# One DMA per k-tile of B in the opening of a 4096-cubed matmul, with two tiles over SyncE and evictions moved to ScalarE

## The chip, the cores and the metric

The kernel runs on one core of one Trainium2 chip. The metric is the device time of one execution in microseconds (us). Times are medians of several runs. Profiles are one execution each; their span is about 2 us shorter than the time of the same run (1789.8 against 1791.62 us before).

PE is TensorE's matmul, PEld its weight load, DVE VectorE, ACT ScalarE, POOL GpSimd, SP SyncE. A "k-tile" is 128 of the 4096 values of K. An eviction moves finished sums out of a PSUM bank, where TensorE leaves them, into SBUF. The granted clock is the share of TensorE's full clock that the throttle let through. A packet is one record of the DMA trace: one contiguous row, for example 4 KB of B.

## The reference

```python
a: (4096, 4096) float32;  b: (4096, 4096) float32;  bias: (4096,) float32
out = tanh(a @ b + bias)          # float32
```

## The kernel before

Both matrices are rounded to fp16 by the DMA that loads them (here these are GpSimd's), A is transposed by DVE in 32x32 blocks (`QP = 32`), and TensorE runs 8,192 matmuls of 128x512 (8,224 in the profile, since the last row tile is done in two halves). K is cut into four quarters (`Q = 4`, `KQ = 1024`), and k-tile `t` consists of 32 rows from each quarter, since that is what the 32x32 transposes of A produce. So a k-tile of B lies in memory as four blocks of 32 rows, 16 MB apart.

```python
P = 128; Q = 4; QP = 32; NB = 512        # NCW = 1024 columns of B at a time, KT = 32 k-tiles
G = 4; KS = 8; WARM = 24                 # opening: two groups of 4 row tiles; k-tiles 0..7 first

def load_b(bt, n0, t0, nt, q):           # one quarter of nt k-tiles
    src = b[ds(q * KQ + t0 * QP, nt * QP), ds(n0, NCW)]
    nc.gpsimd.dma_start(
        out=bt[t0 // TB][ds(q * QP, QP), ds(t0 % TB, nt), :],
        in_=src.rearrange("(t p) n -> p t n", p=QP),         # outermost dimension: 32
    )

def load_b_all(t0, nt):
    for q in range(Q):
        load_b(b_cur, 0, t0, nt, q)

def put_aside(ps, m, j):                 # a PSUM bank of groups 0 and 1 after k-tiles 0..7
    nc.vector.tensor_tensor(
        out=aside(m, j), in0=ps, in1=bias_bc[:, ts(j, NB)], op=mybir.AluOpType.add
    )
# ... (cut)
want_a("g0a", 2, 0, 2 * Q, 0, KS)        # A, group 0, row tiles 0 and 1, k-tiles 0..7 (4 DMAs)
want(lambda: load_b_all(0, 2))
want_a("g0b", 2, 2 * P, 2 * Q, 0, KS)    # A, group 0, row tiles 2 and 3
for t in range(2, KS, 2):
    want(lambda t=t: load_b_all(t, 2))
want(lambda: load_bias(bias_bc, 0))      # 4 KB, read 128 times: 512 KB
want_a("g1a", 2, 4 * P, 2 * Q, 0, KS)
want_a("g1b", 2, 6 * P, 2 * Q, 0, KS)
for t in range(KS, KT, TA):              # the rest of K, 8 k-tiles at a time
    want_a(("g0", t), G, 0, G * Q, t, TA)
    for u in range(t, t + TA, TB):
        want(lambda u=u: load_b_all(u, TB))
# ... (cut: the loads of group 1's rest)
turn(ats[0], "g0a", 0, 0, KS)            # transposes of A
turn(ats[1], "g0a", Q, 0, KS)
across(ps, (0, 1), 0, 2, 0)              # k-tiles 0 and 1, row tiles 0 and 1
turn(ats[2], "g0b", 0, 0, KS)
turn(ats[3], "g0b", Q, 0, KS)
across(ps, (2, 3), 0, 2, 0)
across(ps, range(G), 2, KS - 4, 0)
# ... (cut: group 0 put aside; group 1 the same; then k-tiles 8..31 of both; then the steady loop)
```

While TensorE waits for the first data it runs 24 warm-up matmuls on zeros.

## Time and profile before

| | us |
|---|---|
| time, median of 4 runs (beside the changed kernel) | 1792.15 (1791.02 to 1792.79) |
| steady loop, 7,712 matmuls, busy | 1657.8 (215 ns each) |
| first real matmul | 11.35 |
| group 1 starts | 30.12 |
| k-tile 8 starts | 44.01 |
| last pair of DVE operations starts / span ends | 1785.61 / 1789.8 |

The first two lines are from the page of the kernel before: the busy time of each engine, and the chain of waits by engine. The third is the page's group for the steady loop (busy us and mean ns of one, then idle us ahead of it); the mean of one, 378 ns, includes overlap with the next, so the pace is 1657.8 / 7,712 = 215 ns.

```profile
PE 1779.1 (99%) x8248; PEld 807.4 (45%) x8248; DVE 745.0 (42%) x420; ACT 162.7 (9%) x260; POOL 358.0 (20%) x668
...
PE 95%; DMA 4%; POOL 1%; issue 1%; DVE 0%; ACT 0%; ACTq 0%; DVEq 0%; POOLq 0%
...
L321 PE MATMUL ps<-b,at 128*128 128x512 f16 x7712 | 1657.8, 378 | 0.0
```

TensorE bounds the kernel, and the steady loop has no idle time. Only the opening and the end can move. The timeline of TensorE in the opening of the kernel before has start, length, the instruction, and in brackets the idle time ahead of it and what ended it:

```profile
1.19 7.26 PE L196 MATMUL ps<-zeros 128*128 128x512 f16 x24 [1.19 <-DVE zeros L193]
11.35 3.05 PE L121 MATMUL ps<-b,at 128*128 128x512 f16 x8 [2.90 <-DMA b<-in_b_dram]
15.36 14.06 PE L121 MATMUL ps<-b,at 128*128 128x512 f16 x56 [0.95 <-DVE at L83]
30.12 14.05 PE L121 MATMUL ps<-b,atx 128*128 128x512 f16 x64 [0.71 <-DVE atx L83]
44.01 41.60 PE L121 MATMUL ps<-b,at 128*128 128x512 f16 x192
86.23 41.61 PE L121 MATMUL ps<-b,atx 128*128 128x512 f16 x192 [0.62 <-DVE atx L83]
```

The windows of the kernel before show the granted clock. The columns are the window and its length, then the busy us of PE, PEld, DVE, ACT and POOL with their instructions in brackets, then the granted clock of TensorE, the busy share of the 16 DMA engines, and GB/s written (a share above 1 means packets that overlap):

```profile
12.00:20.00 8.00, 6.96 (x20) 2.15 (x19) 2.37 (x2) 0.00 (x0) 6.50 (x13) 0.58 1.16 200
20.00:30.00 10.00, 9.41 (x44) 4.04 (x42) 3.57 (x6) 0.00 (x0) 7.64 (x14) 1.00 1.34 215
```

After the 2.9 us without work the clock is low: 0.58 on average from 12 to 20 us. Shorter windows have 0.50 from 12 to 18.7 us and 1.00 from 18.8; work had gone on at 15.36. What sets the clock's fall and its return is not shown by this trace. The DMA stream runs at about 200 GB/s written, which is half of what is read (over the whole run, 169.91 MB on the queue of the loads against 337.64 MB read from HBM), and stays there to 80 us (205 GB/s from 30 to 80 us).

### The profile page before, as it was taken

The page shows a single profiled execution, that of the slowest core. Times are in us where ns is not written, and L with a number is a line of the kernel's source. Part 1 is how long each engine was busy: PE and PEld are TensorE (multiplying, and loading weights), DVE is VectorE, ACT ScalarE, POOL GpSimd, SP SyncE. Part 2 cuts the span into 40 slices and gives each one's busy share as a digit, 9 for nine tenths or more (in the row PEclk, how much of TensorE's full clock was granted, in tenths as well). Part 3 has the DMA queues.
Part 4 walks back from the last instruction along what each step waited for, and adds up shares of the span by engine and source line. Part 5 has one row for each costly group of instructions (what it writes and reads, how often), then busy time and mean ns, then how long its engine had stood idle before and what let it go on. Part 6 is the DMA issues. An engine that isn't in the chain of part 4 may idle for free.

```text
span 1789.8 us, 19352 instructions
## 1 busy us (share of the span) xinstructions
PE 1779.1 (99%) x8248; PEld 807.4 (45%) x8248; DVE 745.0 (42%) x420; ACT 162.7 (9%) x260; POOL 358.0 (20%) x668
## 2 busy tenths in 40 slices
PE   8999999999999999999999999999999999999999
PEld 3444444444444444444444444444444444444444
DVE  5463344334433444334433443344334433444341
ACT  0110000000000000000000000000000000000001
POOL 6422222211222211111132222111111111111100
PEclk9999999999999999999999999999999999999999
DMA  9999887665777865655588777555665555655621
GB/s 182 214 189 189 155 159 147 125 132 114 159 147 144 170 140 108 121 119 124 106 168 156 158 142 142 121 112 107 127 120 112 112 113 109 125 112 111 120 70 41
DMA packets 138630, 238.26 MB, mean 133 GB/s; under 512 B 14769, under 2 KB 27569, under 8 KB 138545
## 3 DMA queue, kind: packets, MB, share of 16 engines
q0 software_dynamic: 101248, 169.91, 56.6%
q1 hardware_dynamic: 37296, 67.13, 10.3%
q8 instruction: 64, 1.05, 0.2%
q14 instruction: 22, 0.17, 0.0%
HBM read 337.64 MB, written 67.11 MB: 226 GB/s over the span
## 4 chain that ended last, share of the span: by engine, by line
PE 95%; DMA 4%; POOL 1%; issue 1%; DVE 0%; ACT 0%; ACTq 0%; DVEq 0%; POOLq 0%
PE ps L321 92%; PE ps L121 2%; DMA b<-in_b_dram 2%; DMA an<-in_a_dram 1%; POOL b L66 0%; DMA bias_bc<-in_bias_dram 0%; POOL an L75 0%; DVE atx L83 0%; ACT o_sb L135 0%; DVE o_sb L132 0%; ACTq L354 0%; DVEq L132 0%; POOLq L343 0%
## 5 line engine op out<-in xcount | busy, mean ns | idle before, releaser
L321 PE MATMUL ps<-b,at 128*128 128x512 f16 x7712 | 1657.8, 378 | 0.0
L321 PEld LDWEIGHTS <-at 128*128 128x128 f16 x7712 | 754.6, 98 | 903.3
L132 DVE TENSOR_TENSOR o_sb<-ps,bias_bc 128x512 f32<-128x512 f32 (+1 forms) x243 | 166.4, 686 | 977.8 <-PE ps L321 764.1
L83 DVE STREAM_TRANSPOSE at<-an 128x4096 f16<-128x4096 f16 (+1 forms) x136 | 551.0, 4056 | 26.7 <-DMA an<-in_a_dram 26.7
L75 POOL DMA_DIRECT2D an<-in_a_dram x524 | 282.8, 547 | 1296.6 <-DVE at L83 1224.4
L135 ACT ACTIVATE o_sb<-o_sb 128x512 f32<-128x512 f32 (+1 forms) x243 | 151.5, 624 | 1505.7 <-DVE o_sb L132 1505.7
L66 POOL DMA_DIRECT2D b<-in_b_dram x136 | 73.2, 542 | 55.2 <-PE ps L321 28.6
L121 PE MATMUL ps<-b,at 128*128 128x512 f16 x256 | 58.6, 391 | 3.9 <-DMA b<-in_b_dram 2.9
L121 PE MATMUL ps<-b,atx 128*128 128x512 f16 x256 | 55.7, 379 | 1.3 <-DVE atx L83 1.3
L121 PEld LDWEIGHTS <-at 128*128 128x128 f16 x256 | 25.3, 100 | 37.1 <-issue 5.7
L121 PEld LDWEIGHTS <-atx 128*128 128x128 f16 x256 | 24.8, 98 | 32.2 <-DVE atx L83 2.7
L132 DVE TENSOR_TENSOR spill<-ps,spill 128x512 f32<-128x512 f32 x16 | 10.7, 684 | 25.7 <-PE ps L121 25.4
L135 ACT ACTIVATE spill<-spill 128x512 f32<-128x512 f32 x16 | 10.0, 630 | 117.2 <-DVE spill L132 117.2
L83 DVE STREAM_TRANSPOSE atx<-an 128x1024 f16<-128x1024 f16 (+1 forms) x8 | 18.3, 2295 | 0.0
L155 DVE TENSOR_TENSOR spill<-ps,bias_bc 128x512 f32<-128x512 f32 x16 | 10.1, 670 | 10.0 <-PE ps L121 10.0
L196 PE MATMUL ps<-zeros 128*128 128x512 f16 x24 | 7.3, 476 | 1.2 <-DVE zeros L193 1.2
L196 PEld LDWEIGHTS <-zeros 128*128 128x128 f16 x24 | 2.8, 118 | 5.2 <-issue 2.5
L90 POOL DMA_DIRECT2D bias_bc<-in_bias_dram x4 | 2.3, 563 | 0.1
L135 ACT ACT_TABLE_LOAD x1 | 1.3, 1283 | 0.7 <-PEq L343 0.7
L193 DVE MEMSET zeros<- 128x256 uint32 x1 | 0.3, 272 | 0.9 <-PEq L343 0.9
L343 POOL MEMSET const-float32-0.0<- 128x1 f32 x1 | 0.1, 98 | 0.2 <-issue 0.2
L343 POOL MEMSET const-bfloat16-1.0<- 128x1 bf16 x1 | 0.1, 101 | 0.0
(2 smaller groups left out, 0.2 us busy)
## 6 DMA issues: line engine op xcount, KB each, us to landing
an<-in_a_dram POOLq DMA_DIRECT2D x492, 256.0 KB, 5.4
out_dram<-o_sb SPq DMA_DIRECT2D x239, 256.0 KB, 4.3
b<-in_b_dram POOLq DMA_DIRECT2D x120, 256.0 KB, 8.9
out_dram<-spill SPq DMA_DIRECT2D x16, 256.0 KB, 6.4
an<-in_a_dram POOLq DMA_DIRECT2D x16, 192.0 KB, 7.8
an<-in_a_dram POOLq DMA_DIRECT2D x16, 128.0 KB, 5.7
b<-in_b_dram POOLq DMA_DIRECT2D x16, 128.0 KB, 5.0
bias_bc<-in_bias_dram POOLq DMA_DIRECT2D x4, 512.0 KB, 8.2
```

What stands on the lines that cost most here:

```text
L66: nc.gpsimd.dma_start(out=bt[t0 // TB][ds(q * QP, QP), ds(t0 % TB, nt), :], in_=src.rearrange("(t p) n -> p t n", p=QP),)
L75: nc.gpsimd.dma_start(out=an[ds(q * QP, QP), :, :], in_=src.rearrange("(mb p) k -> p mb k", p=QP),)
L83: nc.vector.transpose(at[:, ds(t0, nt), :].rearrange("P t (mb p) -> P mb t p", p=QP), an[:, ds(mb0, Q), :].rearrange("P mb (t k) -> P mb t ...
L90: nc.gpsimd.dma_start(out=bias_bc, in_=bass.AP(tensor=src.tensor, offset=src.offset, ap=[[0, P], *src.ap]),)
L121: nc.tensor.matmul(ps, at[:, t, :], bt[t // TB][:, t % TB, ts(j, NB)], start=start, stop=stop)
L132: nc.vector.tensor_tensor(out=o_sb[:, piece], in0=ps[:, piece], in1=addend[:, piece], op=mybir.AluOpType.add)
L135: nc.scalar.activation(o_sb[:, piece], o_sb[:, piece], mybir.ActivationFunctionType.Tanh)
L155: nc.vector.tensor_tensor(out=aside(m, j), in0=ps, in1=bias_bc[:, ts(j, NB)], op=mybir.AluOpType.add)
L193: nc.vector.memset(zeros, 0.0)
L196: nc.tensor.matmul(warm, zeros[:, :P], zeros, start=i == 0, stop=i == WARM - 1)
L321: nc.tensor.matmul(ps, at[:, t, :], b_cur[t // TB][:, t % TB, ds(c0, w)], start=t == 0, stop=t == KT - 1,)
L343: nc = _bacc.Bacc("TRN2", target_bir_lowering=False, num_devices=1)
```

## The change

Its intent: start TensorE sooner. Two k-tiles of B leave at once on SyncE as float32 and are rounded by ScalarE; A is ahead of the rest of B on GpSimd; one DMA per k-tile saves GpSimd's issues (0.54 us each); ScalarE empties group 0's banks so that DVE can transpose group 1; three transposes are moved forward; the last stores leave on two queues.

```diff
+    RAW = 2
-    def put_aside(ps, m, j):
+    def put_aside0(ps, m, j):
+        nc.scalar.copy(aside(m, j), ps)
+    def add_bias(m, j):                       # later, on DVE, in SBUF
+        nc.vector.tensor_tensor(out=aside(m, j), in0=aside(m, j), in1=bias_bc[:, ts(j, NB)], ...)
+    def put_aside1(ps, m, j):                 # group 1, as put_aside was
...
+    def b_tile(t):
+        return b.rearrange("(q t p) n -> t q p n", q=Q, p=QP)[t][:, :, ds(0, NCW)]
...
+    raw_b = spill[3].rearrange("P (h x) n -> P h (x n)", h=RAW)
+    for t in range(RAW):
+        nc.sync.dma_start(out=raw_b[:, t, :], in_=b_tile(t))
+        nc.scalar.copy(b_cur[t // TB][:, t % TB, :], raw_b[:, t, :])
...
     want_a("g0a", 2, 0, 2 * Q, 0, KS)
-    want(lambda: load_b_all(0, 2))
     want_a("g0b", 2, 2 * P, 2 * Q, 0, KS)
-    for t in range(2, KS, 2):
-        want(lambda t=t: load_b_all(t, 2))
+    for t in range(RAW, KS):
+        want(lambda t=t: nc.gpsimd.dma_start(out=b_cur[t // TB][:, t % TB, :], in_=b_tile(t)))
+    want_a("g1a", 2, 4 * P, 2 * Q, 0, KS)
     want(lambda: load_bias(bias_bc, 0, nc.gpsimd))
-    want_a("g1a", 2, 4 * P, 2 * Q, 0, KS)
...  # turn1(0), turn1(1) and turn2(0) ahead of the matmuls that they stood behind;
...  # the last stores alternate between nc.sync and nc.scalar
```

The shape of `b_tile(t)`: its source has the dimensions 4 (quarters), 32 (rows), 1024 (columns), so its outermost dimension is 4, where `load_b` had 32.

## The prediction

> **What bounds the kernel now.** TensorE. The chain of waits gives PE 95% of the span, and the busy line 99%. From 128 us on it is untouched: 7,712 matmuls in 1657.8 us, 215 ns each. Only the opening (to about 86 us) and the last 5 us can move. The timeline of the opening shows what is lost there: real matmuls start at 11.35 us, 2.9 us after the warm-up ends at 8.45, waiting for B. The windows show the granted clock at 0.50 from about 12 to 18.3 us, which costs about 3.3 us. Three waits for transposes follow (0.95, 0.71, 0.38 us) and one at 86 us (0.62 us).
>
> A second limit lies behind it: the DMA stream. From 12 to 80 us the windows show a flat 190 to 215 GB/s written (twice that read). Each issue waits for the transfer eight places before; from those issue times the four quarters of B for t=24..27 landed at about 71.0 us, and PE used them at 71.5. So PE can gain only about 0.5 us more than the DMA stream does.
>
> **What the change does.**
> - Two B tiles (512 KB read each) leave on SyncE at about 1 us instead of behind four GpSimd issues of 0.54 to 0.6 us each. The windows 2 to 12 us are short of the later rate by an estimated 0.67 MB written, about 3 us of stream; the extra queue should recover 2.5.
> - ScalarE rounds them, an estimated 1.1 us per tile (its 128x512 operation takes 0.63 us) (A lands at 7.8, then transposes of 1.2 us). Real matmuls could start at 9 to 10 us with the clock still high.
> - ScalarE takes group 0's eight evictions (0.63 us each), so DVE transposes group 1 at once: the 0.71 and 0.38 us waits should go. The eight later bias additions (about 5.5 us of DVE) fall where DVE idles 5.3 us (before 50.4).
> - The transpose ahead of the last four k-tiles removes the 0.62 us wait.
> - Last store on two queues: 0.3 to 0.5 us off the tail.
>
> Good case: PE's 7 to 8 us of possible gain is cut to the stream's 2.5 to 3, plus about 0.5 at 86 us and 0.4 at the end: about 1788.
>
> **The risk.** One DMA per k-tile makes the outermost source dimension 4 instead of 32. [...] If so, both SyncE tiles sit on the same four engines: by the stores' 22.8 GB/s per engine (67 MB in 10.3% of 16 engines), 5.75 us each alone, with A interleaved the second lands near 19 us, PE starts cold and stalls at t=1. Then I estimate 5 to 8 us slower, about 1797. I give this 40%.
>
> **Prediction:** 1789.2 us, range 1786.0 to 1799.0; faster by over 2%: 0.005; within 2%: 0.99; slower by over 2%: 0.005.
>
> **What would show it.** Good case: first real matmul near 9.5 us, granted clock 1.0 throughout, no wait near 86 us, short waits for B inside group 0. Bad case: ScalarE's second rounding ends near 20 us, a long PE wait between t=0 and t=1, clock 0.5 again, and low GB/s in the first 20 us.
>
> **What would make it wrong.** The four-engine rule holding for SyncE but not GpSimd (or the reverse)[...].

One, in "The risk", is a rule for how many DMA engines a load uses. That a load with an outermost dimension of 4 runs on four was my supposition when this was written ("if so", "the four-engine rule"), and p1_alone below is its test. The good case comes to about 1788 us (2.5 to 3, 0.5 and 0.4 us off the kernel before), the bad case to about 1797 (5 to 8 us more), and its 5.75 us per tile are 512 KB at 22.8 GB/s on each of four engines.

## The result, and the profile after

The changed kernel takes 1802.73 us (median of 4 runs, 1801.66 to 1805.0), beside 1792.15 us before. The ratio is 1.0061, 95% interval 1.0044 to 1.0079: slower by 0.6%, which is within the 2% that count as the same. It lies above the predicted range, which ended at 1799.0.

TensorE's timeline in the opening of the changed kernel, to be held against the six lines above:

```profile
1.19 7.21 PE L216 MATMUL ps<-zeros 128*128 128x512 f16 x24 [1.19 <-DVE zeros L213]
21.31 5.80 PE L122 MATMUL ps<-b,at 128*128 128x512 f16 x16 [12.91 <-DVE at L84]
30.42 10.52 PE L122 MATMUL ps<-b,at 128*128 128x512 f16 x48 [3.32 <-DMA b<-in_b_dram]
40.78 13.98 PE L122 MATMUL ps<-b,atx 128*128 128x512 f16 x64
54.59 13.98 PE L122 MATMUL ps<-b,at 128*128 128x512 f16 x64
68.95 13.97 PE L122 MATMUL ps<-b,at 128*128 128x512 f16 x64 [0.39 <-DMA b<-in_b_dram]
84.22 13.97 PE L122 MATMUL ps<-b,at 128*128 128x512 f16 x64 [1.29 <-DMA b<-in_b_dram]
```

The first real matmul starts at 21.31 instead of 11.35 us, group 1 at 40.78 instead of 30.12 (10.7 us later), k-tile 8 at 54.59 instead of 44.01. After that come two waits for B (0.39 and 1.29 us), against one of 0.62 us for a transpose before: about 1.1 us more. The last pair of DVE operations starts at 1797.40 instead of 1785.61, 11.8 us later; the tail after it is 3.5 instead of 4.2 us. So everything is lost before 100 us, and the first 12.91 us wait is not for B: it is for DVE's transposes of A. What they waited for stands in the timeline of all engines of the changed kernel:

```profile
12.68 1.04 ACT L209 CAST b<-spill 128x1024 f16<-128x1024 f32 x1 [10.65 <-DMA spill<-in_b_dram]
13.13 0.71 POOL L223 DMA_DIRECT2D b<-in_b_dram  x1 [7.17 <-DMA an<-in_a_dram]
16.53 0.70 POOL L223 DMA_DIRECT2D b<-in_b_dram  x1 [2.69 <-DMA an<-in_a_dram]
19.12 1.04 ACT L209 CAST b<-spill 128x1024 f16<-128x1024 f32 x1 [5.40 <-DMA spill<-in_b_dram]
19.56 2.80 POOL L223 DMA_DIRECT2D b<-in_b_dram  x4 [2.33 <-DMA an<-in_a_dram]
20.00 2.37 DVE L84 STREAM_TRANSPOSE at<-an 128x1024 f16<-128x1024 f16 x2 [18.87 <-DMA an<-in_a_dram]
```

SyncE's tiles were landed by 12.68 and 19.12 us, and A's first group by 20.00 (before: transposes began at 7.83). A was issued at 1.30 us in both kernels. GpSimd's own issues of B wait too (7.17, 2.69, 2.33 us), because they wait for transfers of A, as the trace has it. That it is the transfer eight places earlier fits the order: eight issues of A go ahead of the first of these waits, and GpSimd's 17th issue (30.66 us, after 7.12 us) is the first that waits for a load of B, the 9th having been the first of B. The windows of the changed kernel say that the DMA engines as a whole were not the limit:

```profile
12.00:20.00 8.00, 0.00 (x0) 0.00 (x0) 0.00 (x0) 1.93 (x2) 1.84 (x3) 0.50 0.40 90
20.00:30.00 10.00, 5.71 (x16) 1.89 (x17) 4.74 (x4) 0.16 (x1) 3.40 (x6) 0.73 1.09 140
```

From 12 to 20 us the 16 DMA engines are 0.40 busy and write 90 GB/s, where they were full and wrote 200 before. TensorE does nothing, and its clock is at 0.50.

### The profile page after: what moved, and what is told of

It reads as the page before. It is cut to its first block, busy times and chain, and to the rows that moved or that the text cites. A ratio compares the mean times of both kernels' runs of the same rounds, so it can differ in the third digit from the quotient of the medians.

```text
span 1800.9 us, 19347 instructions
## 1 busy us (share of the span) xinstructions
PE 1778.1 (99%) x8248; PEld 807.4 (45%) x8248; DVE 745.0 (41%) x420; ACT 168.7 (9%) x270; POOL 353.8 (20%) x658
## 4 chain that ended last, share of the span: by engine, by line
PE 95%; DMA 4%; issue 0%; POOL 0%; ACT 0%; DVE 0%; DVEq 0%; POOLq 0%
PE ps L335 92%; PE ps L122 3%; DMA b<-in_b_dram 3%; DMA an<-in_a_dram 1%; DMA bias_bc<-in_bias_dram 0%; POOL an L76 0%; POOL b L67 0%; ACT o_sb L136 0%; DVE o_sb L133 0%; DVEq L133 0%; POOLq L358 0%
## 5 line engine op out<-in xcount | busy, mean ns | idle before, releaser
L67 POOL DMA_DIRECT2D b<-in_b_dram x120 | 64.8, 544 | 49.4 <-PE ps L335 28.6
L223 POOL DMA_DIRECT2D b<-in_b_dram x6 | 4.1, 680 | 12.3 <-DMA an<-in_a_dram 12.2
L164 DVE TENSOR_TENSOR spill<-ps,bias_bc 128x512 f32<-128x512 f32 x8 | 5.3, 666 | 1.0 <-PE ps L122 1.0
L156 ACT COPY spill<-ps 128x512 f32<-128x512 f32 x8 | 4.0, 623 | 17.8 <-PE ps L122 17.8
L159 DVE TENSOR_TENSOR spill<-spill,bias_bc 128x512 f32<-128x512 f32 x8 | 4.9, 682 | 0.0
```

Of the source, the lines that this page charges most:

```text
L67: nc.gpsimd.dma_start(out=bt[t0 // TB][ds(q * QP, QP), ds(t0 % TB, nt), :], in_=src.rearrange("(t p) n -> p t n", p=QP),)
L156: nc.scalar.copy(aside(m, j), ps)
L159: nc.vector.tensor_tensor(out=aside(m, j), in0=aside(m, j), in1=bias_bc[:, ts(j, NB)], op=mybir.AluOpType.add)
L164: nc.vector.tensor_tensor(out=aside(m, j), in0=ps, in1=bias_bc[:, ts(j, NB)], op=mybir.AluOpType.add)
L223: want(lambda t=t: nc.gpsimd.dma_start(out=b_cur[t // TB][:, t % TB, :], in_=b_tile(t)))
```

## The experiments

The theory: a DMA whose outermost source dimension is 4 runs on four DMA engines. SyncE's two tiles then share four engines with A's parts on them, and A is not landed until its last part is. The rivals: more bytes and one more queue in the opening (contention as such); GpSimd's loads rather than SyncE's; or something else in the change (ScalarE's evictions, the order). Eleven kernels ran; all gave the right result.

### The disputed cost by itself: p1_alone

```diff
+    for g in (2, 4, 8, 16, P):          # 128 rows of 1024: g groups of 128/g rows; P: contiguous rows
+        nc.sync.dma_start(out=raw[:, 0, :], in_=rows(g))
+        nc.scalar.copy(pn, raw[:, 0, :])             # waits for it, and the next load for this
+    for g in (2, 4, 8, 16, P):
+        nc.gpsimd.dma_start(out=pn, in_=rows(g))
+        nc.scalar.copy(raw[:, 1, :], pn)
     # ... then the kernel before
```

> The kernel before, with ten loads of 512 KB ahead of everything, one at a time, each followed by a ScalarE copy: five on SyncE (float32 kept) and five on GpSimd (rounded), whose outermost source dimension is 2, 4, 8, 16 and 128. Theory 1 (the count of DMA engines follows that dimension): on SyncE about 13, 7, 4 to 5, then 3 to 4 us for 16 and 128 alike, and a DMA share of 0.12, 0.25, 0.5, 0.9 while each runs. Rival (shape does not matter, SyncE was slow through contention): all five 3 to 4 us. For GpSimd the theory says the same (13, 7, 5, 4, 4); but if GpSimd is the exception, all five are equal. The time of the kernel grows by the sum, about 50 to 60 us, and the result stays right.

The timeline of ScalarE in this run: each copy waits for one load, the idle time in brackets is that wait, and the outermost dimensions are 2, 4, 8, 16, 128 for SyncE, then the same for GpSimd.

```profile
13.44 1.04 ACT L203 CAST an<-spill 128x1024 f16<-128x1024 f32 x1 [11.41 <-DMA spill<-in_b_dram]
22.68 1.04 ACT L203 CAST an<-spill 128x1024 f16<-128x1024 f32 x1 [8.20 <-DMA spill<-in_b_dram]
30.56 1.04 ACT L203 CAST an<-spill 128x1024 f16<-128x1024 f32 x1 [6.84 <-DMA spill<-in_b_dram]
37.10 1.04 ACT L203 CAST an<-spill 128x1024 f16<-128x1024 f32 x1 [5.50 <-DMA spill<-in_b_dram]
41.82 1.04 ACT L203 CAST an<-spill 128x1024 f16<-128x1024 f32 x1 [3.68 <-DMA spill<-in_b_dram]
56.49 1.04 ACT L206 CAST spill<-an 128x1024 f32<-128x1024 f16 x1 [13.62 <-DMA an<-in_b_dram]
65.50 1.04 ACT L206 CAST spill<-an 128x1024 f32<-128x1024 f16 x1 [7.96 <-DMA an<-in_b_dram]
72.06 1.04 ACT L206 CAST spill<-an 128x1024 f32<-128x1024 f16 x1 [5.53 <-DMA an<-in_b_dram]
78.38 1.04 ACT L206 CAST spill<-an 128x1024 f32<-128x1024 f16 x1 [5.27 <-DMA an<-in_b_dram]
83.69 1.04 ACT L206 CAST spill<-an 128x1024 f32<-128x1024 f16 x1 [4.27 <-DMA an<-in_b_dram]
```

(The first wait started at 2.02 us, after ScalarE's table load; the DMA was issued at 0.75 us, so it took 12.7 us. The other waits include the issue.) For the same 512 KB, a load takes 12.7, 8.2, 6.8, 5.5 and 3.7 us on SyncE, and 13.6, 8.0, 5.5, 5.3 and 4.3 on GpSimd. While the loads with 2, 4 and 8 run on SyncE, windows inside them give DMA shares of 0.12, 0.20 and 0.35, no more than 2, 4 and 8 busy engines out of 16 give (0.125, 0.25 and 0.5). The DMA view of that run has a few small packets beside the rows (4 bytes each in the packet records). I read them as one from each engine used; the reading is mine, and the shares agree with it. These are the counts from 13.5 to 22.68 us, which hold SyncE's load with outermost 4 alone:

```profile
DMA packets 132, 0.52 MB, mean 57 GB/s; under 512 B 4, under 2 KB 4, under 8 KB 132
```

There are 128 rows and 4 small packets. In the same view the load with 2 has 2, the load with 8 has 8, and those with 16 and 128 have 16. So the theory agrees with the times on both queues, and on SyncE with the count. GpSimd's loads look different: with 16 and 128 the views have 16 small packets too, with 2 and 4 many more. From 43.2 to 56.49 us, its load with outermost 2:

```profile
DMA packets 1040, 0.27 MB, mean 20 GB/s; under 512 B 912, under 2 KB 912, under 8 KB 1040
```

912 = 16 + 14 x 64 would be one for each of 16 engines, and for each of 14 idle ones as many as each of the two busy ones has rows. With 4 it is 400 = 16 + 12 x 32. (With 8 only the time from 68.2 us on was looked at, 1.4 us after the issue: 16.) That is arithmetic which fits; the trace does not number the engines. My expectation had the 16- and the 128-row shapes alike; they are not (5.5 and 3.7 us), though both have 16 small packets. The 16 groups lie 4 MB apart and the contiguous rows do not; whether the addresses are the reason was not tried. For the loads on few engines they are not: in the packet records of this run, a 4 KB packet of SyncE took 178 ns in the mean with outermost 4, whose groups lie 16 MB apart as in the change, and 198 ns with contiguous rows. Also missed were the time with 8 (4 to 5 us expected on SyncE), the shares with 4 and 8 (0.25 and 0.5 expected; 0.20 and 0.35 above), and the run's total, 85 us over the kernel before instead of 50 to 60.

### Undoing the shape alone, part by part: e1, e2, e3

```diff
 e1_sync_quarters (and e3):
-        nc.sync.dma_start(out=raw_b[:, t, :], in_=b_tile(t))
+        for q in range(Q):
+            nc.sync.dma_start(out=raw_b[ds(q * QP, QP), t, :],
+                              in_=b[ds(q * KQ + t * QP, QP), ds(0, NCW)])
 e2_pool_quarters (and e3):
-    for t in range(RAW, KS):
-        want(lambda t=t: nc.gpsimd.dma_start(out=b_cur[t // TB][:, t % TB, :], in_=b_tile(t)))
+    for t in range(RAW, KS, 2):
+        want(lambda t=t: load_b_all(t, 2))
```

> The changed kernel with its two SyncE loads cut into four each by K quarter (outermost dimension 32), eight issues; all else as in the change. Theory 1 (the SyncE loads sit on four DMA engines and hold up both themselves and the shares of A on those engines): A lands near 9 us, first real matmul at 9.5 to 11, clock high, kernel within 3 us of before or faster unless GpSimd's six loads have the same fault (then +1 to +4 us). Rival (the extra bytes and the extra queue are what hurts): unchanged, about +10 us.

> The changed kernel with the six GpSimd loads of k-tiles 2 to 7 put back as before (four quarters for each two tiles, outermost 32); SyncE's stay as in the change. Theory 1 with the main fault on SyncE: first real matmul still near 21 us, the 3.3 us wait for k-tile 2 gone or shorter, kernel +7 to +10 us over before. Rival (GpSimd's single loads are the fault): within 3 us of before.

> Both cuts together, so all of the change but its one-DMA-per-k-tile shape. Theory 1: the good case of the prediction, first real matmul at 9.5 to 11 us and 2 to 5 us faster than before (about 1788). Rival (extra queue and bytes): still several us slower than before.

| | us, median | ratio to before, 95% interval | first real matmul |
|---|---|---|---|
| changed kernel | 1802.73 | 1.0061 (1.0044 to 1.0079) | 21.31 |
| e2: SyncE's shape as changed, GpSimd's as before | 1801.47 | 1.0055 (1.0041 to 1.0069) | 22.84 |
| e1: SyncE's shape as before, GpSimd's as changed | 1794.78 | 1.0015 (1.0002 to 1.0028) | 11.70 |
| e3: both as before, all else changed | 1788.63 | 0.9985 (0.9973 to 0.9998) | 11.95 |

The kernel before had 1791.73 us beside the last three. The times fell where I expected them, the first real matmul of e1 and e3 did not (9.5 to 11 us expected), nor did the pace of TensorE stay high in e1 (8 matmuls took 3.43 us from 12.83 on, 429 ns each, against 215 in the steady loop). The first real matmuls of e2 and of e1, in this order:

```profile
22.84 16.48 PE L122 MATMUL ps<-b,at 128*128 128x512 f16 x64 [13.36 <-DVE at L84]
11.70 0.60 PE L122 MATMUL ps<-b,at 128*128 128x512 f16 x2 [2.94 <-DVE at L84]
```

TensorE's timeline in e3:

```profile
1.20 7.12 PE L219 MATMUL ps<-zeros 128*128 128x512 f16 x24 [1.20 <-DVE zeros L216]
11.95 15.64 PE L122 MATMUL ps<-b,at 128*128 128x512 f16 x64 [3.63 <-DVE at L84]
27.42 13.98 PE L122 MATMUL ps<-b,atx 128*128 128x512 f16 x64
41.23 27.79 PE L122 MATMUL ps<-b,at 128*128 128x512 f16 x128
69.49 13.97 PE L122 MATMUL ps<-b,at 128*128 128x512 f16 x64 [0.47 <-DMA b<-in_b_dram]
83.30 41.60 PE L122 MATMUL ps<-b,atx 128*128 128x512 f16 x192
```

The same bytes from the same addresses on the same queues, in pieces whose outermost dimension is 32, turn +10.6 us into -3.1. That refutes contention as such. The cut changes the number of loads too, but p1_alone has the cost without that. The same count can be made in the kernels themselves: these are the packets on SyncE's queue to 22 us, in the changed kernel and in e3.

```profile
q1 hardware_dynamic: 264, 1.05, 16.3%
q1 hardware_dynamic: 384, 1.05, 15.7%
```

Both hold 256 rows of B. The other packets are 8, or 4 for each of two loads, and 128, or 16 for each of eight. The windows of e3 from 12 to 20 us have the DMA full again, against 0.40 and 90 GB/s:

```profile
12.00:20.00 8.00, 7.91 (x30) 3.06 (x31) 3.27 (x3) 0.00 (x0) 6.41 (x12) 0.81 1.12 189
```

Counted from e3's medians, SyncE's shape alone costs 12.8 us, GpSimd's alone 6.2, and both together about 14: they don't add. I take it that where SyncE's tiles already hold up A to 20 us, part of GpSimd's delay is hidden behind that. (The changed kernel ran in other rounds; this last sum is from medians, an estimate.) e2 also shows that A's delay needs nothing of GpSimd's new loads: A's transposes begin at 21.54 us there.

### Why A waits behind B on a shared engine: e4, e9

If SyncE's tiles are on four engines, B's 64 rows per engine should take about 64 x 0.172 us = 11 us there (the trace's length of such a packet), and A's 64 parts of 512 B per engine and group (1,024 parts, if they are spread over 16 engines) 0.06 us each. Why did A take until 20 us? The DMA view of the changed kernel from 12 to 18 us:

```profile
DMA packets 764, 0.53 MB, mean 89 GB/s; under 512 B 525, under 2 KB 649, under 8 KB 764
...
q1 hardware_dynamic: 117, 0.46, 20.3%
```

649 - 525 = 124 packets of A (512 B) against 113 of SyncE's B (4 KB; its queue's 117 hold 4 of 4 bytes): about one of A for each of B, although B's are eight times as large and, at 172 ns against 59, three times as long. (Of the other 525, 521 are 4-byte ones on GpSimd's queue, where p1_alone has many of them for the loads with 2 and 4.) The packet records of this trace show the order too: from 12.5 to 14.5 us B's packets start in four chains, each with one packet of B and one of A every 208 ns. At that pace A's 64 parts take 13.3 us. B's last packet starts at 18.6 us; A then goes from about 20 packets in a us (12 to 17 us) to 94 (19 to 21 us). My reading of these counts is that an engine takes turns between the two queues, packet by packet. Two runs test that.

```diff
 e4_one_tile:
-    RAW = 2
+    RAW = 1                      # k-tile 1 goes by GpSimd, in one DMA
 e9_half_rows:
-        nc.sync.dma_start(out=raw_b[:, t, :], in_=b_tile(t))
+        for h in range(2):       # the same four engines and bytes, 2 KB packets instead of 4 KB
+            nc.sync.dma_start(out=raw_b[:, t, ts(h, NB)], in_=b_tile(t)[:, :, ts(h, NB)])
```

> The changed kernel with one SyncE tile instead of two (k-tile 1 goes by GpSimd in one DMA); the one-DMA-per-k-tile shape kept. In the changed kernel's trace, packets of A (512 B, 60 ns) and of SyncE's B (4 KB, 172 ns) alternate one for one from 12 to 18 us. If that alternation on four shared engines is what holds up A, then with 32 packets of B per engine instead of 64, A's first group lands at 11.5 to 13.5 us instead of 20.0, while B's tile 0 still lands near 12 to 13. First real matmul near 13 to 14.5; k-tile 1 by GpSimd in one DMA then becomes the next wait. Kernel 2 to 8 us faster than the change. If A's delay had another cause (GpSimd issuing eight A transfers in a row), A still lands near 20.

> The changed kernel with each SyncE tile as two loads of half the columns: still four engines and the same bytes, but 2 KB packets, twice as many. If queues on a shared engine take turns packet by packet, A's first group (64 packets of 512 B per engine) passes in 64 turns of about 0.09 + 0.06 us, and lands near 12 to 14.5 us instead of 20.0, while B's second tile is as late as before or later (19 to 22 us). If engines share by bytes, A still lands near 20. First real matmul 13.5 to 16, but k-tile 1 then waits to 20 or later, so the kernel gains little on the change, 0 to 4 us.

e4: A's transposes begin at 15.00 us instead of 20.00, TensorE at 16.31. The direction is right, the size is not (I had 11.5 to 13.5). The first transpose of e4:

```profile
15.00 2.37 DVE L84 STREAM_TRANSPOSE at<-an 128x1024 f16<-128x1024 f16 x2 [13.86 <-DMA an<-in_a_dram]
```

The time is 1800.65 us, ratio 1.0051 (1.0037 to 1.0065), only about 2 us under the change by the medians, with intervals that overlap, because seven k-tiles now come by GpSimd's one-DMA loads and TensorE waits 3.0 us for B and once more 1.26 us for A.

e9: A's transposes begin at 16.95 us, again earlier than 20.00 and later than expected, and so is the first real matmul (18.25 us, 13.5 to 16 expected). Its DMA view from 12 to 18 us:

```profile
DMA packets 859, 0.64 MB, mean 106 GB/s; under 512 B 413, under 2 KB 595, under 8 KB 859
...
q1 hardware_dynamic: 189, 0.37, 18.2%
```

595 - 413 = 182 packets of A in 6 us against 181 of SyncE's B (its queue's 189 hold 8 of 4 bytes): one for one again, and A went 182 / 124 = 1.5 times as fast as in the changed kernel, with B's packets half as large. Sharing by bytes would have left A's rate as it was. So taking turns by packets is what these counts show, and A, with the smaller packets, moves fewer bytes in its turns. The kernel gained nothing clear of noise (1800.88 us, 1.0050, 1.0034 to 1.0065): the second tile of B was rounded at 22.11 us, and TensorE then waited 2.8 us for it. Both landings of A were later than my sums, which took the packet lengths of the quiet stretch after 12 us and nothing for the busy one before it, where SyncE's 4 KB packets took 323 ns in the mean instead of 172 (changed kernel, 6 to 11 us); how much of the delay that explains was not worked out.

### The other parts of the change: e5, e7

```diff
 e5_rest_only: the changed kernel with its loads, and their order, as before
 e7_tail_only: the kernel before, and
+                queues = (nc.sync, nc.scalar) if halves > 1 else (nc.sync,)   # last stores
```

> All of the change except its loads: the kernel before, with loads and their order as before, and ScalarE putting group 0 aside, bias added later, the earlier transposes, and the last stores on two queues. The 0.71, 0.38 and 0.62 us waits of TensorE should be gone and the tail 0.7 us shorter; since B for t=24 lands only about 0.5 us ahead of its use, I expect 1.0 to 1.9 us less than before. If those parts were harmful (ScalarE slower at freeing banks, or the later bias additions delaying transposes), it is slower than before.

> The kernel before with only the last stores spread over SyncE and ScalarE. The time from the last DVE operation's start to the end was 4.2 us before and 3.5 in the changed kernel: I expect 0.5 to 0.8 us less than before, at the edge of what the runs can tell; the trace's tail should show 3.5.

e5: 1790.05 us beside 1791.92; ratio 0.9989 (0.9975 to 1.0002), so the gain of 1.9 us is as large as expected but not clear of noise. Its trace has no wait left at group 1 nor at 86 us (0.71 and 0.62 us before). The parts around the loads are harmless. e7: 1791.84 beside 1791.92, ratio 0.9999 (0.9986 to 1.0011): the tail of its trace is 4.0 us from the start of the last pair of DVE operations (4.2 before), so the second queue gives less than the 0.5 to 0.8 us expected, and nothing that the time shows.

### What bounds the good version: e6, e8, e10

e3 started TensorE at 11.95 us with a low clock (0.50 from 12 to 14 us) and yet met the good case's total. The prediction had said that the DMA stream caps what TensorE can gain.

```diff
 e6_warm40: e3 with
-    WARM = 24
+    WARM = 40
 e8_bias_by_pe: e6, and the first bias not by a 512 KB load:
+    nc.scalar.dma_start(out=bias_row, in_=bias[ds(0, NCW)].rearrange("(x n) -> x n", x=1))
+    nc.vector.tensor_copy(parts[:, 0, :], bias_row)              # fp16
+    nc.vector.tensor_tensor(out=parts[:, 1, :], in0=bias_row, in1=parts[:, 0, :], op=subtract)
+    for j in range(J):                                           # after the warm-up
+        for i in range(2):
+            nc.tensor.matmul(ps, ones, parts[:, i, ts(j, NB)], start=i == 0, stop=i == 1)
+        nc.scalar.copy(bias_bc[:, ts(j, NB)], ps)
 e10_bias_early: e8 with these matmuls between 14 and 20 warm-up ones
```

> The version with both loads cut into quarters, and 40 instead of 24 warm-up matmuls, which fill TensorE's idle time up to its first real matmul at about 11.9 us, so that the granted clock does not fall to 0.5. That gives TensorE about 1.5 us in the opening. If the DMA stream is the limit behind it (B for t=24 already waited for, 0.47 us at 69.5), the wait there grows by the same amount and the time changes by less than 0.5 us; if TensorE alone is the limit, it falls by about 1.5 us.

> The version with quarters and 40 warm-up matmuls, with the first bias not read 128 times from memory (512 KB) but once (4 KB), split by DVE into two fp16 parts and spread over the partitions by four one-row matmuls inside TensorE's idle time. If the DMA stream is what bounds up to k-tile 24, taking 512 KB out of it at about 400 GB/s read brings that tile 1.3 us earlier: 0.8 to 1.3 us less than the version with 40 warm-up matmuls (which had 1788.5), so about 1787.4, and the wait near 69 us is gone or below 0.3 us. If TensorE alone were the limit, no change.

> The version with the bias spread by TensorE, its four one-row matmuls moved into the middle of the warm-up (14 before, 20 after them) so that the first real matmul need not wait for them: it started at 13.9 us there and at 12.6 without them. That version had no wait for B left at k-tile 24, so the DMA stream now leaves room: a start at 11.8 to 12.6 us should show in the time, 0.8 to 1.6 us less than 1787.9. If the stream still bound, the wait near 69 us would come back and the time stay.

| | us | ratio to before, 95% interval | first real matmul | TensorE waits after it |
|---|---|---|---|---|
| e3 | 1788.63 | 0.9985 (0.9973 to 0.9998) | 11.95 | 0.5 us, for B at 69 us |
| e6 | 1788.53 | 0.9983 (0.9970 to 0.9995) | 12.64 | 0.7 us, for B |
| e8 | 1787.91 | 0.9979 (0.9967 to 0.9992) | 13.90 | none |
| e10 | 1787.61 | 0.9979 (0.9965 to 0.9993) | 12.23 | 1.0 us, for A's transposes |

In e6 the clock stays at 1.00 and group 1 starts at 26.46 instead of 27.42 us, and the median time does not move. That the wait at 69 us takes the lead back is not shown: it grows from 0.47 to 0.69 us, and 0.7 of the 0.96 us is still there when the steady loop starts (124.00 against 124.74 us in the two traces). The runs of either version scatter by 2 us. The 40 warm-up matmuls also held up the start, since A's first transpose began at 9.92 us and takes 1.2. This is the list of TensorE's waits of e6 up to 130 us (total, times, longest):

```profile
PE ps L219 <- DVE zeros L216: 1.2, 1, 1.2
PE ps L122 <- DMA b<-in_b_dram: 0.7, 1, 0.7
```

e8 starts later than e6, has no wait for B, and is as fast or a little faster. That fits a stream relieved of 512 KB but doesn't show it: e8 comes to k-tile 24 at about 69.3 us (k-tile 8 starts at 41.53, and 16 k-tiles take 27.79), and in e6 its B was there by 68.75. The gain over e6 (0.6 us) is below what these runs can separate, and below the 0.8 to 1.3 us expected. e10 started at 12.23 us and waited three times for transposes of A (1.6 us in all), whose load landed only at 10.93 us. It has the lowest median of all, 0.2% under the kernel before, but no more than level with e8 and e3 by its interval. It missed the 0.8 to 1.6 us expected over e8. So these three runs leave open what bounds the good version.

## Why the prediction was wrong

- "TensorE bounds; only the opening and the end can move": right. Everything was lost before 100 us.
- "Good case: about 1788": the size was right, but for another kernel and in part by luck. e3, which is the change without its one-DMA shape, has 1788.63 us, though its first real matmul is 0.6 us later than before. Its lead of 2.7 us at group 1 comes from the waits of 0.95 and 0.71 us that are gone and, by an estimate, about 1.7 us from a low clock that ended at about 15.0 us (its windows have 0.50 from 12 to 14 us and 0.74 from 14 to 16) instead of 18.7.
- "Both SyncE tiles sit on the same four engines": right for such loads on SyncE by p1_alone's count (4 small packets for 128 rows) and time (8.2 us, against 3.7 for contiguous rows). On GpSimd the times fit it (8.0 against 4.3).
- **"I give this 40%", and 1789.2 as the point: the first step that failed.** The trace of the kernel before held no load with an outermost dimension of 4, so no number in it could decide, and I put the larger weight on the good case. The bad case, which I put at about 1797, was the nearer one.
- **"Then I estimate 5 to 8 us slower": the second, and the one that put 1802.73 outside the range.** The term for B was nearly exact: "the second lands near 19 us" (rounding began at 19.12), "the clock 0.5 again", low GB/s in the first 20 us, all seen. What the sum lacked was A. I placed the long wait "between t=0 and t=1", so for B alone. It stood before t=0 instead: by the reading above, A's parts on the four shared engines take turns with B's 4 KB packets (124 to 113 from 12 to 18 us), and A landed at 20.00 us instead of about 7.8. TensorE's first real matmul was at 21.31 us, although the first tile of B was rounded by 13.72 us. Then came 3.3 us for k-tile 2, since GpSimd's single loads have the same shape, and were themselves issued late behind A. Measured on e3, SyncE's shape alone is 12.8 us and GpSimd's alone 6.2.
- "Real matmuls could start at 9 to 10 us with the clock still high": wrong even in e3. Beside B, A landed at 10.64 us, TensorE started at 11.95, and the clock fell. What that costs is not shown: e6 keeps the clock and is not faster by the median. Nor is it shown that the stream caps the gain.
- "the 0.71 and 0.38 us waits should go", "removes the 0.62 us wait": right (e3, e5). ScalarE's rounding: estimated 1.1 us, measured 1.04. Later bias additions: estimated 5.5 us, measured 4.9.
- "0.3 to 0.5 us off the tail": too much by time. e7 shows no difference, and its trace 0.2 us (the changed kernel's 0.7).

What stays open: which engines GpSimd's loads use, and how many (the trace does not number them); what sets the fall and the return of the clock; the exact landing of A in e4 and e9; why 16 groups of rows are slower than contiguous rows with as many small packets; and what bounds the good version.

## What to carry to other kernels

Merging several DMAs into one can cost more than the issues it saves: look at the outermost dimension of the source. On SyncE here, loads of 512 KB with 2, 4 and 8 had as many small packets and took 12.7, 8.2 and 6.8 us; with 16 and 128 they had 16 and took 5.5 and 3.7 us, and e3's loads with 32 had 16 each. Keep it at a value like these, even if that means four DMAs: e3 does so and has 1788.63 us, where the changed kernel has 1802.73. When a load is confined to a few engines, don't stop at its own length: here A, on another queue, began to be used at 20.00 us instead of 7.83, and where the two queues took turns (124 packets to 113), the one with small packets moved fewer bytes. In a trace, a low DMA share while everything waits is the sign (0.40 here), and on SyncE the small packets of one load gave a number that agrees with its time and share; on GpSimd, with 912, 400 and 16 of them for 2, 4 and 16, they do not give it directly.
